# Moving the projection's two-input GpSimd steps to VectorE and giving the low-rank sigmoids their own priority in a hybrid SGU, convolution and RWKV-7 block

## The chip, the cores and the metric

One core of one Trainium2 chip runs the whole kernel. The metric is the device time of one execution in microseconds (us); runs are compared by their medians.

## The reference, cut to what matters

The input `x` has 2048 tokens of 1024 features. All arithmetic is float32.

```python
h = rms_norm(x, pre_norm_g)
z = h @ w_in                                  # 1024 x 3712
out_a = spatial_gating(u_a, v_a, ...) * silu(g_a)
out_b = conv_module(val_b, glu_b, ...) * silu(g_b)      # 31 taps, 256 channels
out_c = rwkv7_mix(z_c, ...) * silu(z_g)                 # a scan over 2048 tokens, 8 heads
x = x + rms_norm(concat(out_a, out_b, out_c) @ w_out, post_norm_g)
x = x + (p @ ple_w) * sigmoid(x @ ple_gate_w + ple_gate_b)
```

Inside `rwkv7_mix` the columns of z are shifted by a token (`z + mu * (prev - z)`), and two of them go through low-rank products:

```python
log_w = -DECAY_SCALE * sigmoid(w0 + tanh(wd) @ w_up)
a     = sigmoid(a0 + ad @ a_up)
kk    = k * k_k;  kk = kk * rsqrt(max(sum(kk * kk), 1e-12))     # per head
k     = k * (1 + (a - 1) * k_a)
```

## The kernel before, in words

The program has three stages: the projection with all that prepares the scan (about 0 to 700 us), the scan over chunks of 64 tokens (to about 1190 us), and the output projection with the gate. The change lies in the first.

The projection works in two halves of 1024 tokens. In each, `s_gemm` computes 29 column tiles of 128 columns in the order of the list `ORDER`; two of them (2 and 3) are computed with tokens on the partitions (`gemm_t`, L312), all others by `gemm` (L300). A matmul takes its operands in the format fp32r; to keep float32 accuracy, h and the weights are split into a high and a low part, and a tile takes 48 matmuls of 128x512 (high by high, high by low and low by high for 8 blocks of k and 2 groups of 512 tokens). The result z of a tile has one of two PSUM buffers, which is free again once ScalarE and VectorE have drained it: `shift` does so by L329, L330 and L336, other tiles by a sigmoid, a product or a silu.

`load_w` brings the weights of a tile in the first half: a DMA of the raw tile (L278), the high part by ScalarE (L282), the low part by GpSimd (L283), and two DMAs that store both parts (L285) for the second half, which loads them ready-made. The pool `w` has six buffers, so two sets of raw, high and low: the parts of a tile are written into buffers that an earlier tile's matmuls have just left.

`build_h` makes h. For the first group of 512 tokens VectorE does all of it (L260, L263). For the other groups the tokens lie already transposed in DRAM, and a two-input product by the row of inverse norms (L268) comes first: by VectorE for even groups, by GpSimd for odd ones. `norm_h` puts that engine into `X[g]`.

Per tile there is further work: the convolution's 31 taps for 1024 tokens and two tiles (`s_conv`, L452 on VectorE), the low-rank products (`s_lora` and `s_prep`: the split L430 on GpSimd, the matmuls L469 and L474, the sigmoids L476 and L478 on ScalarE, then the scan L481 on VectorE and the exponentials L484 and L485), the sums over heads (`parts` L231 and L232, matmuls L240), the root L503 and its reciprocal (`recip`, L245), products with r, k and v (L505 to L546), the transposes L537, and the sums L553. `s_sgu` and `s_pw` do the same for the other branches (L595, L603, L637). `s_const` makes the split of the low-rank weights (L165).

Each of these generators yields times in units of a tile, and `at()` sets the priority of what follows. The framework's scheduler puts all instructions into one list per engine by these priorities and by what it expects of their readiness. On the chip each engine then runs its list strictly in that order.

```python
    at(b0 + TG[24] - 5)
    o = shift(12, half, zz, "mk")
```

The value after `at` is the tile's own place (`TG`) less 5: such a step is put ahead of other work that is ready. Names such as z174 or w171 below are buffers with a running number; z174, z193, z198 and z205 are four consecutive tiles of the first half, w171 is the low part of the weights of z198, w188 that of z205, and mk559 is a low part in the second half's last convolution statistics.

## Time and profile before

| what | us |
|---|---|
| median of 3 runs | 1432.69 |
| the runs | 1432.69, 1432.87, 1430.08 |
| the profiled execution | 1433.92 |
| its span | 1432.2 |
| TensorE busy in the span | 1376.5 |
| VectorE busy | 1009.7 |
| ScalarE busy | 579.2 |
| GpSimd busy | 243.6 |

The profile is of one execution. Its span runs from the first to the last instruction that it shows; the execution's own time is 1.7 us longer. Busy time of an engine is the time in which one of its instructions ran. The idle time before an instruction is put down to the instruction of another engine, or the DMA, that it waited for last. In a timeline equal instructions that follow on one another are merged, with their count behind an x; in a row of waits stand the total, how many there were, and the longest.

### The profile page before, as it was taken

The numbers are of one execution on the slowest core, as the hardware profiler recorded it, in microseconds if no ns is written. First come the engines' busy times: TensorE is split into PE (matmuls) and PEld (weight loads), VectorE is DVE, ScalarE is ACT, GpSimd is POOL, SyncE is SP. The second block draws the span as 40 slices with busy tenths as digits, with TensorE's granted clock in tenths as the row PEclk, the third lists the DMA queues.
The fourth block names the chain that finished last, engine by engine and source line by source line (L and its number), as shares of the span: only waits on it lengthen the run. The fifth ranks groups of instructions, "written<-read, shape, count | busy, mean of one in ns | idle before, by whom it ended". The sixth has DMA issues, their size and how long they took to land.

```text
span 1432.2 us, 24400 instructions
## 1 busy us (share of the span) xinstructions
PE 1376.5 (96%) x9701; PEld 1100.4 (77%) x9701; DVE 1009.7 (71%) x2003; ACT 579.2 (40%) x913; POOL 243.6 (17%) x284
## 2 busy tenths in 40 slices
PE   7998999999999999999899999999998989999998
PEld 6876877787898778778677777777776767888887
DVE  6599994885527999777666597789779544545453
ACT  6334445555332344444333554544553543111121
POOL 5431221221501000000111211211221101111120
PEclk9999999999999999999999899999999999999999
DMA  8432466679534458755822833242331534232331
GB/s 335 147 148 89 144 207 193 189 259 298 207 107 157 173 183 249 221 149 187 251 89 78 318 114 105 86 138 82 124 100 57 167 117 147 100 140 100 121 115 44
DMA packets 158311, 223.29 MB, mean 156 GB/s; under 512 B 58236, under 2 KB 108149, under 8 KB 158198
## 3 DMA queue, kind: packets, MB, share of 16 engines
q1 hardware_dynamic: 158066, 221.68, 47.1%
q8 instruction: 76, 1.25, 0.4%
q14 instruction: 37, 0.30, 0.1%
q10 hardware_dynamic: 132, 0.06, 0.0%
HBM read 132.58 MB, written 89.13 MB: 155 GB/s over the span
## 4 chain that ended last, share of the span: by engine, by line
PE 69%; DVE 24%; ACT 3%; issue 2%; DMA 2%; POOL 0%; ACTq 0%; POOLq 0%; DVEq 0%
PE z L300 32%; PE z L1167 12%; PE z L1054 6%; DVE inv L452 6%; PE c L1144 3%; DVE inv L873 3%; DVE inv L878 3%; PE z L312 2%; PE m L820 2%; PE m L240 1%; DVE mk L245 1%; DVE L L976 1%; DVE inv L861 1%; PE m L1123 1%; PE c L943 1%
## 5 line engine op out<-in xcount | busy, mean ns | idle before, releaser
L300 PE MATMUL z<-h,w 128*128 128x512 f32 x2592 | 631.6, 398 | 1.5 <-ACT zl L336 1.4
L300 PEld LDWEIGHTS z<-h,w 128*128 128x128 f32 x2592 | 485.0, 189 | 119.3 <-issue 6.0
L1054 PE MATMUL z<-h,w 128*128 128x512 f32 x768 | 203.5, 408 | 0.6 <-DVE w L1041 0.6
L452 DVE SCALAR_TENSOR_TENSOR inv<-inv,vc,inv 128x1024 f32<-128x1024 f32 x120 | 171.7, 1449 | 1.4
L1054 PEld LDWEIGHTS z<-h,w 128*128 128x128 f32 x768 | 138.4, 190 | 31.2 <-DVE w L1041 1.0
L283 POOL TENSOR_TENSOR w<-w,w 128x1024 fp32r<-128x1024 f32 x26 | 71.6, 2755 | 238.3 <-PE z L300 172.5
L1167 PE MATMUL z<-L,w 128*128 128x512 f32 (+1 forms) x384 | 96.3, 394 | 0.0
L1151 ACT ACTIVATE inv<-inv 128x512 f32<-128x512 f32 (+1 forms) x33 | 20.5, 620 | 182.1 <-DVE inv L1150 182.1
L1167 PE MATMUL z<-h,w 128*128 128x512 f32 (+1 forms) x384 | 93.1, 390 | 0.8 <-DVE inv L1150 0.8
L873 DVE TENSOR_TENSOR inv<-inv,inv 128x48 f32<-128x48 f32 (+23 forms) x464 | 85.7, 219 | 2.3
L878 DVE TENSOR_TENSOR inv<-inv,inv 128x48 f32<-128x48 f32 (+23 forms) x464 | 84.2, 217 | 1.2
L1167 PEld LDWEIGHTS z<-h,w 128*128 128x128 f32 x384 | 71.3, 188 | 17.4 <-DVE inv L1150 1.2
L1150 DVE TENSOR_TENSOR inv<-z,L 128x512 f32<-128x512 f32 (+1 forms) x32 | 21.8, 683 | 89.1 <-PE z L1167 89.1
L1167 PEld LDWEIGHTS z<-L,w 128*128 128x128 f32 x384 | 70.4, 188 | 15.3
L1111 POOL TENSOR_TENSOR inv<-inv,pg 128x1024 f32<-128x1024 f32 x16 | 38.3, 2397 | 218.0 <-DMA inv<-mx_s 168.1
L245 DVE RECIPROCAL mk<-mk 128x256 f32<-128x256 f32 x40 | 65.8, 1708 | 12.1 <-ACT mk L637 8.0
L825 DVE TENSOR_TENSOR mk<-m,mask 128x512 f32<-128x512 f32 x58 | 37.5, 683 | 35.9 <-PE m L820 31.7
L978 POOL TENSOR_TENSOR ri<-ri,pc 128x256 f32<-128x256 f32 x31 | 19.5, 629 | 236.1 <-DVE L L976 225.9
L312 PE MATMUL z<-w,h 128*128 128x256 f32 x384 | 52.5, 293 | 0.9 <-ACT h L262 0.9
L312 PEld LDWEIGHTS z<-w,h 128*128 128x128 f32 x384 | 50.3, 197 | 3.0 <-ACT h L262 1.6
L829 ACT COPY inv<-mk 32x128 f32<-32x128 f32 x128 | 37.8, 295 | 35.9 <-DVE mk L825 33.1
L282 ACT CAST w<-w 128x1024 fp32r<-128x1024 f32 x26 | 27.3, 1048 | 60.1 <-DMA w<-in_w_in_dram 44.4
(245 smaller groups left out, 1959.0 us busy)
## 6 DMA issues: line engine op xcount, KB each, us to landing
w_s<-w SPq DMA_DIRECT2D x58, 512.0 KB, 3.4
w<-w_s SPq DMA_DIRECT2D x58, 512.0 KB, 5.3
w<-in_w_in_dram SPq DMA_DIRECT2D x26, 512.0 KB, 3.8
L<-in_x_dram SPq DMA_DIRECT2D x16, 512.0 KB, 7.3
ar_s<-L SPq DMA_DIRECT2D x16, 512.0 KB, 4.7
wo_s<-w SPq DMA_DIRECT2D x16, 512.0 KB, 4.5
L<-ar_s SPq DMA_DIRECT2D x32, 256.0 KB, 3.1
L<-bk_s SPq DMA_DIRECT2D x32, 256.0 KB, 3.9
```

Source lines behind the costliest of these rows:

```text
L245: nc.vector.reciprocal(t[:, g * 256:(g + 1) * 256], t[:, g * 256:(g + 1) * 256])
L283: nc.gpsimd.tensor_tensor(out=ws[1], in0=wr, in1=ws[0], op=ALU.subtract)
L300: nc.tensor.matmul(z[:, g * 512:(g + 1) * 512], lhsT=ws[a][:, k * 128:(k + 1) * 128], rhs=h[:, b, k, :], start=(n == 0), stop=(n == 23))
L312: nc.tensor.matmul(z[:, i * 256:(i + 1) * 256], lhsT=h[:, b, k, i * 128:(i + 1) * 128], rhs=ws[k // 4][a][:, (k % 4) * 256:(k % 4 + 1) * 2 ...
L452: nc.vector.scalar_tensor_tensor(out=ac, in0=y[:, i:i + HT], scalar=col(V_CW + 2 * i + ct), in1=ac, op0=ALU.mult, op1=ALU.add)
L829: nc.scalar.copy(g["g"][32 * q:32 * q + 32, 0, 4 * ci:4 * ci + 4, :], mk[32 * q:32 * q + 32, par, :, s0:s0 + 32])
L873: nc.vector.tensor_tensor(out=tmp[:, o:o + n, :m], in0=tl[:, lo:hi, m:m + 1].to_broadcast([128, n, m]), in1=ml[:, m, :m].unsqueeze(1).to_b ...
L878: nc.vector.tensor_tensor(out=tl[:, lo:hi, :m], in0=tl[:, lo:hi, :m], in1=tmp[:, o:o + n, :m], op=ALU.add)
L1054: nc.tensor.matmul(mx[:, nh * 512:(nh + 1) * 512], lhsT=oT[a][:, k, :], rhs=wo[k // 4][:, b, k % 4, nh * 512:(nh + 1) * 512], start=(k == ...
L1111: nc.gpsimd.tensor_tensor(out=x2, in0=x2, in1=pg[0], op=ALU.mult)
L1144: nc.tensor.matmul(pp, lhsT=pT[:, a, k, :], rhs=gw[8 + k][b][:, nh * 512:(nh + 1) * 512], start=(n == 0), stop=(n == 5))
L1167: nc.tensor.matmul(z, lhsT=xT[a][:, k, :], rhs=gw[k][b][:, sl], start=(k == 0 and n == 0), stop=(k == 7 and n == 2))
```

## The change

GpSimd's four kinds of two-input instructions in the projection become VectorE's: the split of the low-rank weights (L165), the product L268 of odd groups, the weight split L283 and the split L430. In `s_prep` the two sigmoids are given the priority of the tile's place less 5, and the priority goes back to its old value behind them.

```diff
--- before.py
+++ after.py
@@ -162,7 +162,7 @@
             hi = slice(64 * j, 64 * j + 64)
             for lo in (0, 64):
                 nc.scalar.copy(wup_h[lo:lo + 64, j], wup_t[hi])
-            nc.gpsimd.tensor_tensor(out=wup_l[hi], in0=wup_t[hi], in1=wup_h[hi, j], op=ALU.subtract)
+            nc.vector.tensor_tensor(out=wup_l[hi], in0=wup_t[hi], in1=wup_h[hi, j], op=ALU.subtract)
         nc.sync.dma_start(out=pw_t, in_=pw_w.rearrange("(k p) n -> p k n", p=128))
         yield 1.5
         cps = mps((128, 2, 128))
@@ -223,7 +223,7 @@
             nc.sync.dma_start(out=xk, in_=x_t[256 * k2:256 * k2 + 256, g * 512:(g + 1) * 512]
                               .rearrange("(k p) t -> p k t", p=128))
             xt += [xk[:, 0], xk[:, 1]]
-        X[g] = (xt, rb[:, 1], nc.vector if g % 2 == 0 else nc.gpsimd)
+        X[g] = (xt, rb[:, 1])
 
     def parts(src, eng):
 
@@ -262,10 +262,10 @@
                     nc.scalar.copy(h[:, 0, k4, sl], xb)
                     nc.vector.tensor_tensor(out=h[:, 1, k4, sl], in0=xb, in1=h[:, 0, k4, sl], op=ALU.subtract)
             return h
-        xt, rb, eng = xr
+        xt, rb = xr
         for k in range(8):
             at(t + 0.05 * k)
-            eng.tensor_tensor(out=xt[k], in0=xt[k], in1=rb, op=ALU.mult)
+            nc.vector.tensor_tensor(out=xt[k], in0=xt[k], in1=rb, op=ALU.mult)
             nc.scalar.activation(h[:, 0, k, :], xt[k], AF.Identity, scale=col(V_PRE + k))
             nc.vector.scalar_tensor_tensor(out=h[:, 1, k, :], in0=xt[k], scalar=col(V_PRE + k),
                                            in1=h[:, 0, k, :], op0=ALU.mult, op1=ALU.subtract)
@@ -280,7 +280,7 @@
         for wr, ct in zip(wrs, cts):
             ws = [new("w", dt=F32R) for _ in range(2)]
             nc.scalar.copy(ws[0], wr)
-            nc.gpsimd.tensor_tensor(out=ws[1], in0=wr, in1=ws[0], op=ALU.subtract)
+            nc.vector.tensor_tensor(out=ws[1], in0=wr, in1=ws[0], op=ALU.subtract)
             for j in range(2):
                 nc.sync.dma_start(out=w_s[ct, :, j], in_=ws[j].bitcast(F32))
             r.append(ws)
@@ -427,7 +427,7 @@
             wa = new(tag, dt=F32R)
             hi, lo = slice(64 * j, 64 * j + 64), slice(64 - 64 * j, 128 - 64 * j)
             nc.scalar.copy(wa[hi], o[hi])
-            nc.gpsimd.tensor_tensor(out=wa[lo], in0=o[hi], in1=wa[hi], op=ALU.subtract)
+            nc.vector.tensor_tensor(out=wa[lo], in0=o[hi], in1=wa[hi], op=ALU.subtract)
             st["wa"].append(wa)
 
     def s_conv(half, ct, st):
@@ -473,9 +473,12 @@
                 hi = slice(64 * j, 64 * j + 64)
                 nc.tensor.matmul(lps[j], lhsT=wup_l[hi, p * 128:(p + 1) * 128], rhs=wa[j][hi, sl],
                                  start=False, stop=True)
+
+            at(b0 + TG[12 + p] - 5)
             nc.scalar.activation(sw[:, 8 * g:8 * g + 8, 1:65], lps[0].rearrange("p (c s) -> p c s", s=64),
                                  AF.Sigmoid, bias=col(V_W0 + p))
             nc.scalar.activation(ic[:, g * 512:(g + 1) * 512], lps[1], AF.Sigmoid, bias=col(V_A0 + p))
+            at(b0 + TG[12 + p] - 0.6)
 
         ep = sw
         nc.vector.tensor_tensor_scan(ep.rearrange("p c s -> p (c s)"), rst.rearrange("p c s -> p (c s)"),
```

Lines up to 475 are the same in both kernels; from there the changed kernel's numbers are larger by 2 or 3 (L501 becomes L504, L503 L506, L537 L540, L546 L549, L553 L556, L595 L598).

The first place is in the first half, behind the end of z174, on VectorE. Before, the list went by L517 and the drain of z167 to the clamp L501 of the head sums and the reciprocals:

```order
L452 SCALAR_TENSOR_TENSOR inv105_894<-inv104_890,vc_116,inv105_894 128x1024
L232 TENSOR_TENSOR mk154_1303<-mk152_1300,mk153_1302 128x1024
L452 SCALAR_TENSOR_TENSOR inv105_894<-inv104_890,vc_116,inv105_894 128x1024
L517 TENSOR_TENSOR L172_1433<-L139_1155,L128_1070 128x8x64
L330 SCALAR_TENSOR_TENSOR L168_1419<-z167_1369,vc_116,L168_1419 128x1023
L452 SCALAR_TENSOR_TENSOR inv105_894<-inv104_890,vc_116,inv105_894 128x1024 x2
L501 TENSOR_SCALAR mk152_1300<-m155_1306 128x512
L501 TENSOR_SCALAR mk152_1300<-m156_1310 128x512
L452 SCALAR_TENSOR_TENSOR inv105_894<-inv104_890,vc_116,inv105_894 128x1024
L245 RECIPROCAL mk152_1300<-mk152_1300 128x256 x4
L452 SCALAR_TENSOR_TENSOR inv105_894<-inv104_890,vc_116,inv105_894 128x1024
L232 TENSOR_TENSOR mk164_1353<-L117_979,mk163_1352 128x1024
```

Now:

```order
L232 TENSOR_TENSOR mk154_1303<-mk152_1300,mk153_1302 128x1024
L529 TENSOR_TENSOR L112_916<-L122_1044,L112_916 128x1024
L549 SCALAR_TENSOR_TENSOR L117_979<-L117_979,vc_116,L122_1044 128x1024
L452 SCALAR_TENSOR_TENSOR inv105_894<-inv104_890,vc_116,inv105_894 128x1024 x2
L283 TENSOR_TENSOR w171_1428<-w169_1425,w170_1427 128x1024
L504 TENSOR_SCALAR mk152_1300<-m155_1306 128x512
L504 TENSOR_SCALAR mk152_1300<-m156_1310 128x512
L452 SCALAR_TENSOR_TENSOR inv105_894<-inv104_890,vc_116,inv105_894 128x1024 x2
L245 RECIPROCAL mk152_1300<-mk152_1300 128x256 x4
L452 SCALAR_TENSOR_TENSOR inv105_894<-inv104_890,vc_116,inv105_894 128x1024
L232 TENSOR_TENSOR mk164_1353<-L117_979,mk163_1352 128x1024
L283 TENSOR_TENSOR w188_1547<-w186_1544,w187_1546 128x1024
```

The split of w171 stands ahead of the clamp, and that of w188 behind the reciprocals. On ScalarE the root L503 (now L506), which these reciprocals need, stood ahead of the cast of w187:

```order
L336 COPY zl_126<-z167_1369 128x1
L503 ACTIVATE mk152_1300<-mk152_1300 128x1024
L539 COPY mk157_1328<-m158_1329 128x512
L231 CAST mk163_1352<-L117_979 128x1024
L539 COPY mk157_1328<-m159_1335 128x512
L282 CAST w187_1546<-w186_1544 128x1024
```

Now:

```order
L336 COPY zl_126<-z167_1369 128x1
L282 CAST w187_1546<-w186_1544 128x1024
L506 ACTIVATE mk152_1300<-mk152_1300 128x1024
L542 COPY mk157_1328<-m158_1329 128x512
L231 CAST mk163_1352<-L117_979 128x1024
L542 COPY mk157_1328<-m159_1335 128x512
```

The cast has moved ahead of the root, the two copies L539 and the high part L231.

The second place is where VectorE's list comes to the drain of z193. Before:

```order
L525 TENSOR_TENSOR mk152_1300<-mk152_1300,L134_1090 128x1024
L523 TENSOR_TENSOR L151_1296<-L151_1296,mk129_1071 128x1024
L481 SCALAR_TENSOR_TENSOR L179_1520<-inv1_98,L179_1520 128x1040
L452 SCALAR_TENSOR_TENSOR inv105_894<-inv104_890,vc_116,inv105_894 128x1024
L526 TENSOR_TENSOR L134_1090<-L151_1296,L134_1090 128x1024
L546 SCALAR_TENSOR_TENSOR L139_1155<-L139_1155,vc_116,L151_1296 128x1024
L330 SCALAR_TENSOR_TENSOR L194_1619<-z193_1569,vc_116,L194_1619 128x1023
L232 TENSOR_TENSOR mk190_1554<-L139_1155,mk189_1553 128x1024
```

Now, with the third split and the gate product of z198 ahead of that drain:

```order
L528 TENSOR_TENSOR mk152_1300<-mk152_1300,L134_1090 128x1024
L526 TENSOR_TENSOR L151_1296<-L151_1296,mk129_1071 128x1024
L484 SCALAR_TENSOR_TENSOR L179_1520<-inv1_98,L179_1520 128x1040
L452 SCALAR_TENSOR_TENSOR inv105_894<-inv104_890,vc_116,inv105_894 128x1024
L529 TENSOR_TENSOR L134_1090<-L151_1296,L134_1090 128x1024
L549 SCALAR_TENSOR_TENSOR L139_1155<-L139_1155,vc_116,L151_1296 128x1024
L283 TENSOR_TENSOR w197_1627<-w195_1624,w196_1626 128x1024
L598 TENSOR_TENSOR mk175_1495<-z198_1636,mk175_1495 128x1024
L452 SCALAR_TENSOR_TENSOR inv105_894<-inv104_890,vc_116,inv105_894 128x1024
L330 SCALAR_TENSOR_TENSOR L194_1619<-z193_1569,vc_116,L194_1619 128x1023
L232 TENSOR_TENSOR mk190_1554<-L139_1155,mk189_1553 128x1024
```

So w197's split, L598 (before L595) and a tap come between L549 and L330, and L595 stood behind L232 before.

The third place is the end of the second half on TensorE, where the last sums of the convolution statistics (mk559, L240) stand. Before, with matmuls of the tile z588 behind them:

```order
L300 MATMUL z588_4922<-h346_2839,w545_4650 128x512
L300 MATMUL z588_4922<-h346_2839,w544_4649 128x512 x2
L240 MATMUL m561_4741<-mk559_4737,onesm_84 128x512
L240 MATMUL m562_4747<-mk559_4737,onesm_84 128x512
L300 MATMUL z588_4922<-h346_2839,w545_4650 128x512
L300 MATMUL z588_4922<-h346_2839,w544_4649 128x512 x2
L300 MATMUL z588_4922<-h346_2839,w545_4650 128x512
L300 MATMUL z588_4922<-h346_2839,w544_4649 128x512 x2
L300 MATMUL z588_4922<-h346_2839,w545_4650 128x512
L300 MATMUL z588_4922<-h346_2839,w544_4649 128x512 x2
L300 MATMUL z588_4922<-h346_2839,w545_4650 128x512
L300 MATMUL z588_4922<-h346_2839,w544_4649 128x512
L537 MATMUL m569_4833<-ident_78,L553_4724 128x128 x4
```

Now, with all of these ahead of them:

```order
L300 MATMUL z588_4922<-h346_2839,w545_4650 128x512
L300 MATMUL z588_4922<-h346_2839,w544_4649 128x512 x2
L300 MATMUL z588_4922<-h346_2839,w545_4650 128x512
L300 MATMUL z588_4922<-h346_2839,w544_4649 128x512
L240 MATMUL m561_4741<-mk559_4737,onesm_84 128x512
L240 MATMUL m562_4747<-mk559_4737,onesm_84 128x512
L540 MATMUL m569_4833<-ident_78,L553_4724 128x128 x4
L540 MATMUL m570_4839<-ident_78,L553_4724 128x128 x4
L240 MATMUL m573_4852<-mk571_4848,ones64_83 128x512
```

What follows both is the transposes L537 (L540) and the last sums over heads.

## Rows read from the trace of the kernel before

**Rows 1.** The page's busy line: busy us of each engine, share of the span, instructions.
```profile
PE 1376.5 (96%) x9701; PEld 1100.4 (77%) x9701; DVE 1009.7 (71%) x2003; ACT 579.2 (40%) x913; POOL 243.6 (17%) x284
```

**Rows 2.** TensorE's waits, 36 to 250 us: what it waited for, us in total, times, longest.
```profile
PE m L240 <- ACT mk L231: 3.6, 2, 2.7
PE m L240 <- DVE mk L232: 1.7, 1, 1.7
PE z L300 <- ACT zl L336: 1.4, 1, 1.4
PE c L469 <- ACT L L476: 0.3, 1, 0.3
```

**Rows 3.** Two windows at half clock: start:end, length, busy us (instructions) by engine, clock, DMA.
```profile
143.50:146.90 3.40, 3.40 (x9) 2.75 (x9) 3.40 (x3) 1.07 (x2) 0.77 (x1) 0.50 0.00 0
...
696.50:703.30 6.80, 4.73 (x42) 4.40 (x44) 4.33 (x7) 3.48 (x3) 0.00 (x0) 0.50 0.95 265
```

**Rows 4.** GpSimd's groups by form: count, busy us, mean ns, idle before, releasers.
```profile
L283 POOL TENSOR_TENSOR w<-w,w 128x1024 fp32r<-128x1024 f32 x26 | 71.6, 2755 | 238.3 <-PE z L300 172.5 <-ACT w L282 55.2 <-DMA bk_s<-mk 7.0
L268 POOL TENSOR_TENSOR L<-L,mk 128x512 f32<-128x512 f32 x16 | 26.0, 1658 | 13.5 <-DMA w_s<-w 13.5
...
L430 POOL TENSOR_TENSOR pg<-mk,pg 64x1024 fp32r<-64x1024 f32 x2 | 6.5, 3273 | 0.1
...
L165 POOL TENSOR_TENSOR yc<-mk,ri 64x512 fp32r<-64x512 f32 x2 | 2.9, 1442 | 0.2
```

**Rows 5.** VectorE's groups by form, same columns.
```profile
L452 DVE SCALAR_TENSOR_TENSOR inv<-inv,vc,inv 128x1024 f32<-128x1024 f32 x120 | 171.7, 1449 | 1.4
...
L232 DVE TENSOR_TENSOR mk<-mk,mk 128x1024 fp32r<-128x1024 f32 x12 | 14.6, 1220 | 8.5 <-ACT mk L231 8.0 <-PE m L240 0.4
...
L553 DVE TENSOR_TENSOR L<-m,L 128x512 f32<-128x512 f32 x16 | 10.3, 683 | 8.7 <-PE m L240 8.7
```

**Rows 6.** VectorE's timeline around 182 us: start, length, instruction.
```profile
181.02 3.42 DVE L546 SCALAR_TENSOR_TENSOR L<-L,vc,L 128x1024 f32<-128x1024 f32 x1
```

**Rows 7.** GpSimd's timeline, 160 to 226 us: start, length, instruction, idle before and releaser.
```profile
180.07 3.28 POOL L283 TENSOR_TENSOR w<-w,w 128x1024 fp32r<-128x1024 f32 x1 [7.05 <-DMA bk_s<-mk]
195.30 2.40 POOL L283 TENSOR_TENSOR w<-w,w 128x1024 fp32r<-128x1024 f32 x1 [11.95 <-PE z L300]
```

**Rows 8.** Windows of the first 700 us, columns as in Rows 3.
```profile
184.00:226.00 42.00, 39.05 (x168) 29.43 (x168) 39.21 (x35) 23.66 (x28) 7.25 (x4) 1.00 0.71 205
...
250.00:430.00 180.00, 180.00 (x885) 146.44 (x884) 109.30 (x109) 82.79 (x103) 42.37 (x20) 1.00 0.63 212
430.00:680.00 250.00, 250.00 (x1094) 197.59 (x1093) 209.69 (x204) 101.97 (x106) 9.06 (x10) 1.00 0.61 188
```

**Rows 9.** VectorE's timeline in the head, 0 to 40 us.
```profile
10.05 3.23 DVE L263 TENSOR_TENSOR h<-L,h 128x512 fp32r<-128x512 f32 x2
```

**Rows 10.** ScalarE's timeline, 186 to 215 us.
```profile
199.36 1.05 ACT L282 CAST w<-w 128x1024 fp32r<-128x1024 f32 x1 [2.83 <-DMA w<-in_w_in_dram]
```

**Rows 11.** VectorE's timeline, 188 to 222 us.
```profile
194.66 6.59 DVE L245 RECIPROCAL mk<-mk 128x256 f32<-128x256 f32 x4
...
215.56 2.31 DVE L481 TENSOR_TENSOR_SCAN L<-inv,L 128x1040 f32<-128x1040 f32 x1
...
221.30 1.27 DVE L330 SCALAR_TENSOR_TENSOR L<-z,vc,L 128x1023 f32<-128x1023 f32 x1
```

**Rows 12.** TensorE's timeline, 200 to 228 us.
```profile
225.92 2.25 PE L300 MATMUL z<-h,w 128*128 128x512 f32 x9
```

**Rows 13.** TensorE's timeline, 680 to 700 us.
```profile
687.29 2.73 PE L300 MATMUL z<-h,w 128*128 128x512 f32 x11
```

**Rows 14.** TensorE's waits, 640 to 710 us, columns as in Rows 2.
```profile
PE m L240 <- DVE mk L232: 2.6, 1, 2.6
PE m L603 <- DVE L L553: 2.1, 1, 2.1
PE m L240 <- ACT mk L231: 1.2, 1, 1.2
```

## The prediction, made before the changed kernel ran

> **What bounds the kernel now.** The page's busy line comes first: TensorE works 96% of the span, VectorE 71%, GpSimd 17% [rows 1]. The change touches the projection stage (0 to about 700 us) alone, so only what TensorE misses there can be won: its waits and its time at a lower clock. The waits of TensorE from 36 to 250 us sum to 3.6 + 1.7 + 1.4 + 0.3 = 7.0 us, and each ends on VectorE or on ScalarE work that stood behind VectorE [rows 2]. After the longest wait the granted clock is 0.50 for 3.4 us, the 1.2 GHz level instead of 2.4, with TensorE busy throughout, which loses half of it, 1.7 us [rows 3]. So 8.7 us are to be had in the first half. From 250 to 680 us TensorE is busy without a gap while VectorE has 71 and 40 us free [rows 8]: there an instruction more on VectorE costs nothing. At the end of the second half there are 2.6 + 2.1 + 1.2 = 5.9 us of waits [rows 14] and 6.8 us at 0.50 [rows 3].
>
> Why VectorE is late in the first half is read from two timelines side by side. L546 starts at 181.02 and takes 3.42 us; the weight split L283 on GpSimd runs from 180.07 to 183.35 [rows 6, 7]. For the same amount of data VectorE takes 1.2 to 1.3 us elsewhere (L232 1.22, L330 1.27) [rows 5, 11]. The same shows in the means: the 120 convolution taps L452 average 1.449 us, 0.18 above 1.27, hence 120 x 0.18 = 21 us lost by them alone [rows 5].
>
> **The change part by part.** Removed from GpSimd are 29 splits L283 (26 of 2.755 us, three more of the head), 16 steps L268 of 1.658, four L430 and two L165 [rows 4]. VectorE gets them at its own prices, 1.22 us for 128x1024 (L232) and 0.68 for 128x512 (L553) [rows 5]: 29 x 1.22 + 16 x 0.68 + 4 x 1.22 + 2 x 0.68 = 52.5 us. It gets back at least the 21 us of the taps; at most it gets back the moved instructions' whole GpSimd time, 71.6 + 26.0 + 2 x 6.5 + 2.9 and some 7 for the head's three splits = about 120 us, if VectorE had stood still through all of it. The busy sum thus does not decide. The Trainium skill (Perfetto Trace Analysis, Optimizing Scalar/DVE Operations) says that moving work between GpSimd and VectorE might not help, as they share a read port; by that alone the change would be worth about nothing, and rows 6 and 7 agree that they block one another. What decides is where the added instructions stand in VectorE's queue.
>
> *Up to the end of tile z174 (about 195 us).* I laid VectorE's new order end to end with the durations above, letting each L283 wait for the end of the gemm whose buffer it reuses, as GpSimd's did (172.5 us in all [rows 4]). The drains L330 of z116, z121 and z138 then come 6 us or more before TensorE needs their buffers, and so do the sums of L240. All waits before this point go: 1.41 and 2.67, the 1.70 behind L232 [rows 2], and the 1.7 us of clock [rows 3]: -7.5 us.
>
> *From the end of z174 to the start of z205.* Here a wait comes instead. On GpSimd the split of w171 waited 11.95 us for the end of z174 and ended nobody's work [rows 7]. Now it stands on VectorE ahead of L501 (first fence of the change); what is queued behind it are L501, the taps, the reciprocals L245, and 20 more instructions until L330 of z193 frees the buffer that z205 needs (second fence). With tau = 0 at z174's end (195.30 [rows 7]), 1.2 us for each full step and 0.6 for a half one: split, two L501, two taps, 4.8. L245 needs ScalarE's L503, which now stands behind the cast of w187, whose data came at 199.36, tau 4.1 [rows 10]; 4.1 + 1.05 + 1.06 = 6.2. L245 6.6 [rows 11], 12.8. Then tap, L232, split, L505, tap: 18.8. Three halves, tap, L521, two halves: 24.3. Tap, L525, L523: 27.9; the scan 2.3 [rows 11]: 30.2; tap, L526, L546, the third split, L595, tap: 37.4; L330: 38.6. Starts overlap a little, so I take 38 us. Before, L330 of z193 started at tau 26.0 [rows 11] and z205 at 30.6 [rows 12], of which 0.29 + 0.96 = 1.25 were waits [rows 2]; z205 could start at 29.35 were VectorE in time. The new wait is 38 - 29.35 = 8.7 us, less those 1.25: **+7.4 us**. It lies open, because the c and m matmuls ahead of z205 wait on ScalarE behind the same scan. The bounds: 6 us (all starts overlapping, L503 in time) and 10.
>
> *The clock in that wait.* No row shows what an 8.7 us wait does to it; 2.7 us was followed by 3.4 us at 0.50, the 5.9 us by 6.8 us [rows 3]. Half of these is 1.7 and 3.4; I take **+2.5**, keeping 0 to 3.4.
>
> *Head.* Three splits now stand between the steps that make h: 3 x 1.22 = 3.7 us more. Without GpSimd beside them two L263 that took 3.23 us [rows 9] take 1.3, and one L202 wins about as much: 3.8 us less. I take **0**, -1.5 to +1.5.
>
> *End of the second half.* The pair L240 of mk559 stood ahead of 11 matmuls L300 that took 2.73 us [rows 13]; now it stands behind them (third fence). From this pair hang L637, L245, L232 and L603, which are waited for in the open [rows 14], and the 11 matmuls no longer fill any of it: 11 x 0.23 = **+2.5 us**, 0 to +4.
>
> *The rest.* L268 of the second half and L430 of the second half lie in 250 to 680 us, covered by VectorE's free 71 and 40 us [rows 8]; they would cost at most 8 x 0.68 + 2 x 1.22 = 7.9 us if that cover were gone. L165 has VectorE idle around it. The stores of the low parts (L285) follow the splits on SP's queue, later by at most the new wait; they are read again in the second half, hundreds of us later. GpSimd's queue keeps only memsets. The sigmoids L476/L478 move by one or two places on ScalarE, behind the same matmuls: 0, with -1 to +1.
>
> Sum: -7.5 + 7.4 + 2.5 + 0 + 2.5 = **+4.9 us**. The profiled execution took 1433.92 us (span 1432.2, so 1.7 around it); with the change 1438.8. That execution is 1.2 above the median of 1432.69, so I forecast 1437.6. With the bounds, 1433.5 to 1442.
>
> **The rivals.**
> (1) *VectorE set free.* The Trainium skill (SBUF — State Buffer, SBUF: two separate sides) has it that a VectorE instruction with two SBUF operands and a GpSimd one that reads SBUF exclude each other for a whole instruction. Rows 6 and 7 agree. As a mechanism of this kernel: if blocked time is most of what VectorE was late by, the tau chain ends before tau 30, all 8.7 us go, and with the +2.5 at the end the time is 1432.69 - 6.2 = 1426.5. For it: VectorE was 93% busy from 184 to 226 us (39.21 of 42) [rows 8]. Against it: the chain above already uses unblocked durations. 0.23.
> (2) *Every split a wait.* Each L283 of the first half holds VectorE's queue until a gemm ends; if a gemm's worth of VectorE work exceeds the 11 us between two ends not once but at two or three tiles, the wait of z205 comes again. One more is +8.7 and clock: 1447. It decides from the point where VectorE is still behind when z205 ends; after it VectorE had much idle time, so 0.12.
> (3) *The two cancel.* The chain ends at tau 33 to 35, by a start earlier than I see: then -7.5 + 3 + 2.5 + a little clock = about -1, 1431.7. This is also the case that the change does little because TensorE's matmuls moved to later places. 0.15.
>
> **How the numbers follow.** The forecast has 0.5. A measurement of this kernel can tell about 0.2%, 2.9 us, from no change. Faster: rival 1 and a little of 3, 0.25. Same: most of 3 and the lower end of the forecast, 0.21. Slower: the rest of the forecast and rival 2, 0.54. The range from 1426 to 1443 takes in rivals 1 and 3 and leaves out rival 2 and the tails.
>
> **What would show it.** Right: in the trace of the changed kernel no tap L452 above 1.4 us; no TensorE wait from 100 to 185 us and no 0.50 there; VectorE waiting for TensorE ahead of L283; an idle stretch of TensorE of 7 to 10 us ahead of z205, ended by L330, L231 or the sigmoid of c184, near 220 us; the waits at 690 us at about 8.5. Wrong: z205 starting by 219 us with no such gap (rival 1); a second such gap after 240 us (rival 2).

## The result, and the profile after

The changed kernel takes 1440.35 us (median of 4 runs, 1439.07 to 1441.86); the kernel before, run again beside it, 1432.78 us. The ratio is 1.0061 [1.0046, 1.0076], so it is slower by 0.6%. The forecast of 1437.6 us had the direction, and its range holds the time. The profiled execution took 1439.07 us with a span of 1437.4, 5.2 us more than the span before. The busy line of the page, as in [rows 1]:

```profile
PE 1376.4 (96%) x9701; PEld 1100.4 (77%) x9701; DVE 1005.8 (70%) x2054; ACT 582.6 (41%) x915; POOL 123.9 (9%) x233
```

GpSimd's busy time falls from 243.6 to 123.9 us, while VectorE, with 51 instructions more, is busy for 3.9 us less. Two groups of VectorE's lines by form show the larger part of why (count, busy us, mean ns, idle time ahead and what ended it):

```profile
L452 DVE SCALAR_TENSOR_TENSOR inv<-inv,vc,inv 128x1024 f32<-128x1024 f32 x120 | 151.0, 1277 | 1.2
...
L283 DVE TENSOR_TENSOR w<-w,w 128x1024 fp32r<-128x1024 f32 x26 | 31.8, 1222 | 30.8 <-PE z L300 9.4 <-PE z L312 9.4 <-issue 6.6
```

The 120 taps fall from 1449 to 1277 ns [rows 5], 120 x 0.172 = 20.7 us given back; 26 splits come in at 1.22 us, 31.8 us. What outweighs the rest is spread over other steps that GpSimd no longer holds up: the eight L549, for one, take 10.2 us in all where they took 14.5 as L546. The second row holds the price that the busy time hides: VectorE stands idle for 30.8 us ahead of splits, 18.8 of them for the gemm whose weight buffer they reuse.

TensorE's waits from 36 to 250 us (what it waited for, us in total, times, longest), as in [rows 2]:

```profile
PE c L469 <- ACT mk L480: 4.7, 1, 4.7
PE z L300 <- ACT mk L595: 3.5, 1, 3.5
PE m L240 <- ACT mk L231: 1.8, 1, 1.8
PE z L312 <- ACT mk L438: 1.1, 1, 1.1
```

They sum to 11.1 us against 7.0. The 2.7, 1.7 and 1.4 of before are gone; the 0.3 + 1.0 ahead of z205 have become 4.7 + 1.8, and the 3.5 ahead of z198 is new. These three lie on TensorE's way from z174 to z205. Its timeline there (start, length, instructions, idle time ahead and what ended it):

```profile
195.82 1.03 PE L540 MATMUL m<-ident,L 128*128 128x128 f32 x8
...
204.79 6.23 PE L300 MATMUL z<-h,w 128*128 128x512 f32 x19 [3.52 <-ACT mk L595]
...
226.18 0.80 PE L469 MATMUL c<-mk,ri 128*128 128x512 f32 x1 [4.68 <-ACT mk L480]
...
229.49 1.22 PE L240 MATMUL m<-mk,ones 128*128 128x512 f32 x2 [1.80 <-ACT mk L231]
230.51 3.68 PE L300 MATMUL z<-h,w 128*128 128x512 f32 x11
```

z174 ended at 188.32 (195.40 before), so the forecast's tau is the time less 188.2, the start of the split behind it. From there VectorE's timeline, same columns:

```profile
188.19 1.23 DVE L283 TENSOR_TENSOR w<-w,w 128x1024 fp32r<-128x1024 f32 x1 [1.49 <-PE z L300]
...
194.35 6.59 DVE L245 RECIPROCAL mk<-mk 128x256 f32<-128x256 f32 x4 [1.22 <-ACT mk L506]
...
215.97 2.32 DVE L484 TENSOR_TENSOR_SCAN L<-inv,L 128x1040 f32<-128x1040 f32 x1
...
225.18 1.27 DVE L330 SCALAR_TENSOR_TENSOR L<-z,vc,L 128x1023 f32<-128x1023 f32 x1
```

The split waits 1.49 us for z174, as forecast; the reciprocals start at tau 6.2 (forecast 6.2), the scan at 27.8 (27.9), L330 of z193 at 37.0 (37.4). But L330, which ended at 226.45, is not what ended the waits. ScalarE's timeline shows what did:

```profile
196.46 0.59 ACT L542 COPY mk<-m 128x512 f32<-128x512 f32 x1 [2.15 <-PE m L540]
...
202.42 1.28 ACT L595 ACT_TABLE_LOAD   x1 [3.95 <-DMA v_s<-mk]
...
219.10 0.59 ACT L542 COPY mk<-m 128x512 f32<-128x512 f32 x1 [4.03 <-PE m L540]
...
222.06 1.06 ACT L487 ACTIVATE L<-L 128x1024 f32<-128x1024 f32 x1
...
225.44 0.69 ACT L480 ACTIVATE mk<-c,vc 128x512 f32<-128x512 f32 x1
...
228.41 1.03 ACT L231 CAST mk<-L 128x1024 fp32r<-128x1024 f32 x1
```

The silu L595 that drains the z buffer for z198 waits 3.95 us for the store v_s to free an mk buffer. That store reads the copies L542, and those wait for the transposes L540, which TensorE now reaches later in its list. So z198 starts 3.52 us late. Further on the copy L542 waits 4.03 us for the next transposes, and L487 (which needs the scan), L480 and L231 follow it in ScalarE's queue: they end TensorE's 4.68 and 1.80. z205 starts at 230.51, tau 42.3; before it was 225.92 [rows 12].

Windows of the four stretches up to 715 us in which the granted clock was 0.50, the 1.2 GHz level (start:end, length, busy us and instructions by engine, clock, DMA share, GB/s), as in [rows 3]:

```profile
41.50:44.90 3.40, 3.29 (x8) 1.99 (x7) 3.30 (x8) 0.99 (x2) 0.00 (x0) 0.50 0.00 0
205.30:208.70 3.40, 3.40 (x9) 2.69 (x9) 3.40 (x6) 2.69 (x3) 0.00 (x0) 0.50 0.86 324
225.80:232.60 6.80, 4.62 (x9) 3.05 (x10) 3.74 (x4) 4.73 (x7) 0.00 (x0) 0.50 0.75 231
700.30:713.90 13.60, 7.74 (x52) 5.96 (x53) 11.13 (x12) 4.58 (x4) 0.00 (x0) 0.50 0.66 189
```

One stretch follows each wait or group of waits; the first (41.50) stands in the head. At the end of the second half TensorE's waits, as in [rows 14]:

```profile
PE m L240 <- DVE mk L232: 4.2, 1, 4.2
PE m L606 <- DVE L L556: 1.6, 1, 1.6
PE m L240 <- ACT mk L231: 1.0, 1, 1.0
PE m L540 <- ACT mk L640: 0.6, 1, 0.6
```

That is 7.4 us where 5.9 stood, and 13.6 us at half clock where 6.8 stood.

The account of the two profiled executions, by the start of the same work (us, before and after):

| work on TensorE | before | after | change so far |
|---|---|---|---|
| z85 | 55.62 | 57.40 | +1.8 |
| z138 | 128.14 | 128.11 | 0.0 |
| end of z174 | 195.40 | 188.32 | -7.1 |
| z205 | 225.92 | 230.51 | +4.6 |
| the gemm at the end of the first half | 360.82 | 367.48 | +6.7 |
| the last gemm ahead of the waits at 690 us | 677.33 | 684.13 | +6.8 |
| the next gemm behind them | 708.85 | 718.61 | +9.8 |
| end of the span | 1432.18 | 1437.35 | +5.2 |

The 4.6 us that come back after 709 us lie in code that the change doesn't touch. From that next gemm to the end it took 723.3 us before, 718.7 after, and 720.3 to 723.9 in the profiles of the experiments below, so it varies between executions. Its last 2 us left out, it held 17.1 us at 0.50 before and 10.2 after, which with TensorE busy is up to 3.4 of the 4.6 us; the rest lies in its short waits and isn't traced further. So the profiles differ by 5.2 us where the medians differ by 7.6: the profiled execution of the kernel before lay 1.1 us above its median, that of the changed kernel 1.3 below.

### The profile page after: what moved, and what is told of

Same layout as the page of the kernel before. It is cut to its first block, busy times and chain, and to the rows that moved or that the text cites. A ratio compares the mean times of both kernels' runs of the same rounds, so it can differ in the third digit from the quotient of the medians.

```text
span 1437.4 us, 24384 instructions
## 1 busy us (share of the span) xinstructions
PE 1376.4 (96%) x9701; PEld 1100.4 (77%) x9701; DVE 1005.8 (70%) x2054; ACT 582.6 (41%) x915; POOL 123.9 (9%) x233
## 3 DMA queue, kind: packets, MB, share of 16 engines
q8 instruction: 76, 1.25, 0.4%
## 4 chain that ended last, share of the span: by engine, by line
PE 79%; DVE 14%; ACT 4%; DMA 2%; issue 1%; SPq 0%; ACTq 0%; DVEq 0%
PE z L300 41%; PE z L1170 12%; PE z L1057 6%; DVE inv L876 3%; PE z L312 3%; PE c L1147 3%; DVE inv L881 3%; PE m L823 2%; PE m L240 1%; DVE L L979 1%; DVE inv L864 1%; PE m L1126 1%; PE c L946 1%; DMA w<-in_gate_w_dram 1%; PE c L474 1%
## 5 line engine op out<-in xcount | busy, mean ns | idle before, releaser
L452 DVE SCALAR_TENSOR_TENSOR inv<-inv,vc,inv 128x1024 f32<-128x1024 f32 x120 | 151.0, 1277 | 1.2
L245 DVE RECIPROCAL mk<-mk 128x256 f32<-128x256 f32 x40 | 65.9, 1709 | 20.2 <-ACT mk L506 11.1
L329 ACT ACTIVATE L<-z,om 128x1024 f32<-128x1024 f32 x24 | 26.8, 1115 | 85.8 <-PE z L300 85.8
L282 ACT CAST w<-w 128x1024 fp32r<-128x1024 f32 x26 | 27.3, 1050 | 77.9 <-DMA w<-in_w_in_dram 58.4
L283 DVE TENSOR_TENSOR w<-w,w 128x1024 fp32r<-128x1024 f32 x26 | 31.8, 1222 | 30.8 <-PE z L300 9.4
```

Source lines behind the costliest of these rows:

```text
L245: nc.vector.reciprocal(t[:, g * 256:(g + 1) * 256], t[:, g * 256:(g + 1) * 256])
L452: nc.vector.scalar_tensor_tensor(out=ac, in0=y[:, i:i + HT], scalar=col(V_CW + 2 * i + ct), in1=ac, op0=ALU.mult, op1=ALU.add)
```

## The experiments

The theory, called queue theory in the expectations: list order decides. A two-input step on VectorE takes less than half the time (a split 1.22 us instead of 2.76), but takes its wait for a gemm along into VectorE's queue, and the order around it changes on all engines. Rivals: VectorE has too much to do in that stretch (capacity), or the sigmoids' new place costs. Ratios are to the kernel before in the same series.

**1. The moves without the sigmoids.**

```diff
-            at(b0 + TG[12 + p] - 5)
             nc.scalar.activation(sw[...], ..., AF.Sigmoid, ...)
             nc.scalar.activation(ic[...], ..., AF.Sigmoid, ...)
-            at(b0 + TG[12 + p] - 0.6)
```

> The changed kernel without the sigmoids' priority; all four kinds of instruction stay on VectorE. Queue theory (the loss comes from where the weight splits stand in VectorE's queue): the lists around z174 to z205 are those of the changed kernel, so 1440 us within 2 us, a gap of about 10 us ahead of z205 in all (3.5, 4.7 and 1.8 in the trace of the change). Sigmoid theory (the earlier sigmoids hold up ScalarE's casts and roots there): 1433 us or less, with the 4.7 us wait behind the second sigmoid gone.

Measured: 1439.04 us, 1.0041 [1.0025, 1.0056]. TensorE's waits from 36 to 250 us are the changed kernel's to a tenth of a us: 4.7, 3.5, 1.8 and 1.1.

z205 starts at 228.53; the 3.4 us at half clock at 41.5 us are missing here, and z85 starts at 55.44, so the head itself costs nothing. The sigmoids' priority doesn't bring these waits; it moves nothing at all. In the two traces TensorE, VectorE, ScalarE and GpSimd run the same operations on the same tiles (by their names without the numbers) in the same order from the first to the last.

**2. The sigmoids alone** (the kernel before with their priority).

```diff
+            at(b0 + TG[12 + p] - 5)
             nc.scalar.activation(sw[...], ..., AF.Sigmoid, ...)
             nc.scalar.activation(ic[...], ..., AF.Sigmoid, ...)
+            at(b0 + TG[12 + p] - 0.6)
```

> The kernel before with the sigmoids' priority alone. Queue theory: as before, 1433 us within 2 us, with the waits of 1.4, 2.7 and 1.7 us in the first half still there. Sigmoid theory: slower by 3 us or more, with a wait behind L480 ahead of z205.

Measured: 1432.88 us, 0.9998 [0.9987, 1.0008]. The order on all four engines is that of the kernel before. So that part of the change does nothing, and the whole loss is the moves'. The waits that were expected again are there only in part: the 1.4 us for L336 are missing and the longest for L231 is 3.4 us, not 2.7, so some of a profile's waits differ between executions of the same lists.

**3. The changed kernel with the splits L283 on GpSimd.**

```diff
-            nc.vector.tensor_tensor(out=ws[1], in0=wr, in1=ws[0], op=ALU.subtract)
+            nc.gpsimd.tensor_tensor(out=ws[1], in0=wr, in1=ws[0], op=ALU.subtract)
```

> The changed kernel with the weight splits L283 back on GpSimd; the 16 products, the splits of the low-rank product and of its weights stay on VectorE. Queue theory: the gap ahead of z205 goes (waits there of 1 to 2 us as before), the waits of the kernel before at 126 to 185 us come back in part because GpSimd blocks VectorE again, and the end of the second half keeps its later pair L240 (+3 us): 1433 to 1437 us. Capacity theory (VectorE simply has too much work): between the two as well, about 1435, but with the gap ahead of z205 only shortened. Where the end of the second half has waits of about 6 us as before, its 3 us came from the splits.

Measured: 1437.29 us, 1.0034 [1.0022, 1.0047], at the upper end of what the queue theory gave. The waits behind L480 and L595 are gone, but waits of 4.0 (1.7 of them right ahead of z205), 1.1, 1.1 and 1.1 us stand at other places, the taps are back at 1423 ns, and the end of the second half has 7.6 us of waits, so its loss doesn't come from the splits. They are not the whole loss: L268, L430 and the rest, moved without them, cost 0.34% (4.9 us). In this profile 2.1 us of that arise at the end of the second half and about as much in the first 70 us, where 3.4 us stand at half clock.

**5. The splits alone on VectorE** (the kernel before, one line).

```diff
-            nc.gpsimd.tensor_tensor(out=ws[1], in0=wr, in1=ws[0], op=ALU.subtract)
+            nc.vector.tensor_tensor(out=ws[1], in0=wr, in1=ws[0], op=ALU.subtract)
```

> The kernel before with all 29 weight splits on VectorE and nothing else moved. The split of w171 now stands behind L501, the cast of w187 behind the root, and L330 of z193 comes some 6 us sooner after the end of z174 than in the changed kernel; the last pair L240 of the second half keeps its 11 matmuls behind it. Queue theory: the 7 us won before z174's end stay, 3 us of waits remain ahead of z205, nothing is lost at the end of the second half: 1428 to 1432 us. Capacity theory (35 us more work on VectorE, wherever it stands): 1437 to 1440 us.

Measured: 1440.09 us, 1.0041 [1.0024, 1.0057]; the gain that I expected was missed. z205 starts at 220.62 as it should. The loss stands 160 us later. TensorE's timeline there, then VectorE's:

```profile
383.11 11.10 PE L300 MATMUL z<-h,w 128*128 128x512 f32 x36 [5.87 <-DVE w L283]
```
```profile
368.32 12.53 DVE L268 TENSOR_TENSOR L<-L,mk 128x512 f32<-128x512 f32 x8 [8.08 <-ACT mk L219]
380.77 2.28 DVE L283 TENSOR_TENSOR w<-w,w 128x1024 fp32r<-128x1024 f32 x1
```

and GpSimd's beside it:

```profile
368.86 13.11 POOL L268 TENSOR_TENSOR L<-L,mk 128x512 f32<-128x512 f32 x8 [32.13 <-ACT mk L219]
```

A split stands behind eight L268 that run beside GpSimd's eight (12.53 us for eight; in the changed kernel one L268 takes 0.69 us), itself takes 2.28 us beside GpSimd, and a gemm waits 5.87 us for it; 6.8 us at half clock go with it. The forecast looked at no such place. It is not the second rival's mechanism either: this split does not hold VectorE's queue for a gemm, it is late because of what stands ahead of it. With experiment 3 the two parts make 0.34% + 0.41%, and both together 0.61%; the intervals are too wide to tell whether they add, but the stalls of the parts stand for the most part at other places than those of the whole.

The start of z205 shows something more: here the splits of w171, w188 and w197 are VectorE's too, and it comes at 220.62. They delay z205 in the order that they have with the other moves, not by being on VectorE.

**4 and 8. Which splits.** The changed kernel with the splits of the first half from step 15 on back on GpSimd (4), and with those of steps 15 to 17 alone back (8):

```diff
-            nc.vector.tensor_tensor(out=ws[1], in0=wr, in1=ws[0], op=ALU.subtract)
+            (eng or nc.vector).tensor_tensor(out=ws[1], in0=wr, in1=ws[0], op=ALU.subtract)
...
-                    W[0, ct] = load_w(ct, tag="inv" if n == 2 else "w")
+                    W[0, ct] = load_w(ct, tag="inv" if n == 2 else "w",
+                                      eng=nc.gpsimd if n >= 15 else None)
```

(in 8: `nc.gpsimd if 15 <= n <= 17 else None`)

> The changed kernel, but the weight splits from the tile z198 on (14 of 29) are GpSimd's, the first 15 VectorE's. Queue theory: the waits from 100 to 185 us stay away and the 10 us of waits ahead of z205 fall to 0 to 2 us with their 5 us at half clock: 1440 - 10 - 2.5 = 1427 to 1430 us. Capacity theory: VectorE gives up only 3.5 us of work before z205, so the gap falls by about 3.5 us: 1436 us.

> The changed kernel with only three of its 29 splits back on GpSimd, those of w171, w188 and w197, which stand between the ends of z174 and z198. Queue theory: those three make the gap, so this equals the run with 14 late splits on GpSimd (1432 us) within 1.5 us. Capacity theory: 3 x 1.2 us of VectorE's time come back, at most 4 us: 1436 us.

Measured: 1432.29 us, 0.9996 [0.9985, 1.0007], and 1438.77 us, 1.0032 [1.002, 1.0044]. z205 starts at 219.50 and 219.63, some 9 us earlier than in experiment 1, whose head has no half clock either: sending three splits back takes the delay of z205 away. But both still have 5.7 us of waits before 250 us and the loss at 690 us. So 4 misses the 1427 to 1430 us: 6.4 us ahead of the kernel before at z205, it is 3.3 us ahead at 674 us, and the end of the second half takes 2.6 of these. And 8, which I expected within 1.5 us of 4, loses some 5.6 us at the end of the first half: the gemm there starts 3.9 us later than in 4, and 3.4 us at half clock stand behind it. TensorE's timeline of 8 there, then ScalarE's:

```profile
354.43 1.98 PE L665 MATMUL c<-inv,jk 128*128 128x512 f32 x4
360.38 6.45 PE L300 MATMUL z<-h,w 128*128 128x512 f32 x20 [3.97 <-ACT pg L657]
```
```profile
354.20 1.04 ACT L282 CAST w<-w 128x1024 fp32r<-128x1024 f32 x1 [6.51 <-DMA w<-in_w_in_dram]
358.01 1.28 ACT L657 ACT_TABLE_LOAD   x1 [2.76 <-DMA ab_s<-pg]
359.31 1.02 ACT L657 ACTIVATE pg<-z 128x1024 f32<-128x1024 f32 x1
```

L657 drains the buffer that the gemm at 360.38 needs, and stands behind a cast whose weights came late and a store that frees pg. In the changed kernel the same wait is 1.4 us, in 4 it is 0.2. Moving three splits changed the order 140 us later.

**11. Capacity or order.** The changed kernel with the splits of steps 15 to 17 made twice. The second writes the same values.

```diff
-            nc.vector.tensor_tensor(out=ws[1], in0=wr, in1=ws[0], op=ALU.subtract)
+            for _ in range(times):
+                nc.vector.tensor_tensor(out=ws[1], in0=wr, in1=ws[0], op=ALU.subtract)
...
-                    W[0, ct] = load_w(ct, tag="inv" if n == 2 else "w")
+                    W[0, ct] = load_w(ct, tag="inv" if n == 2 else "w", times=2 if 15 <= n <= 17 else 1)
```

> The changed kernel with the splits of w171, w188 and w197 made twice, which changes no value: 3.5 us more work on VectorE between z174's end and z205. Capacity theory: the drain of z193 ends 3.5 us later, at 230 us, and the run takes 1443 to 1445 us. Queue theory: the time follows what the lists put ahead of z205; here the scheduler leaves the root ahead of the cast of w187 again and puts the pair L240 of z205's head sums behind 31 matmuls of z205, so z205 starts right behind the drain, at 227 to 230 us and not later than in the changed kernel: 1437 to 1441 us.

Measured: 1439.3 us, 1.0052 [1.004, 1.0064]. With more work on VectorE L330 of z193 starts at 220.51 and z205 at 226.03, about 1 us earlier than expected. In experiment 1, which like this run has no half clock at 41.5 us, they start at 223.20 and 228.53. TensorE's waits, line numbers one higher:

```profile
PE c L470 <- ACT mk L481: 5.0, 2, 3.7
PE z L301 <- ACT mk L596: 3.5, 1, 3.5
```

Capacity falls: it asked for a z205 that is 3.5 us later, and more work there gave an earlier one, partly because the pair L240 of z205's head sums now stands behind its first matmuls. The added instructions led to another order on the engines, and that order decided; the 3.5 us of z198 stay. The time itself can't be told from the changed kernel's (0.52% against 0.61%).

**6 and 7. A part of the moves.** The kernel before with the splits of steps 4 to 14 and L430 of the first half on VectorE (6); the same with L430 of the second half too (7: `nc.vector` for both halves):

```diff
-            nc.gpsimd.tensor_tensor(out=ws[1], in0=wr, in1=ws[0], op=ALU.subtract)
+            (eng or nc.gpsimd).tensor_tensor(out=ws[1], in0=wr, in1=ws[0], op=ALU.subtract)
...
-                    W[0, ct] = load_w(ct, tag="inv" if n == 2 else "w")
+                    W[0, ct] = load_w(ct, tag="inv" if n == 2 else "w",
+                                      eng=nc.vector if 4 <= n < 15 else nc.gpsimd)
...
-            nc.gpsimd.tensor_tensor(out=wa[lo], in0=o[hi], in1=wa[hi], op=ALU.subtract)
+            (nc.vector if half == 0 else nc.gpsimd).tensor_tensor(out=wa[lo], in0=o[hi], in1=wa[hi], op=ALU.subtract)
```

> The kernel before with the splits of the 11 tiles from n = 4 to 14 of the list and the first half's split L430 on VectorE; all else stays on GpSimd, the later splits too. Both losses that the queue theory names are left out: no split stands in VectorE's queue after z174, and the last pair L240 keeps its place. Queue theory: 1424 to 1428 us, the fastest of all. If a loss of another kind goes with the moves (the head, VectorE's load), 1431 or more.

> As the run before it, with the second half's L430 on VectorE too, two instructions more. They are covered by VectorE's free time; but the scheduler then puts the last pair L240 behind all 11 matmuls of its tile. If the place of that pair costs the 3 us at the end of the second half, this run is 2.5 to 3.5 us above the run before it, with the TensorE waits near 690 us at 7.5 instead of 6 us; if not, the two are equal.

Measured: 1432.64 us, 0.9994 [0.9984, 1.0003], and 1434.74 us, 1.0009 [1.0, 1.0018]. 6 misses its gain: waits of 1.8, 1.6 and 1.2 us stand before 250 us and one of 1.5, for a split on GpSimd, later. Its lead over the kernel before is 4.0 us at z205, 2.1 at the end of the first half and nothing at 677 us. 7 is a clean test of the forecast's last term, since it differs from 6 by two instructions. TensorE's timeline at the end of the second half, of 6 and then of 7:

```profile
686.82 0.61 PE L240 MATMUL m<-mk,onesm 128*128 128x512 f32 x2
687.28 2.73 PE L300 MATMUL z<-h,w 128*128 128x512 f32 x11
...
695.69 0.74 PE L240 MATMUL m<-mk,ones 128*128 128x512 f32 x2 [2.65 <-DVE mk L232]
```
```profile
686.07 2.25 PE L300 MATMUL z<-h,w 128*128 128x512 f32 x9
688.16 0.62 PE L240 MATMUL m<-mk,onesm 128*128 128x512 f32 x2
...
697.03 1.22 PE L240 MATMUL m<-mk,ones 128*128 128x512 f32 x2 [4.44 <-DVE mk L232]
```

In 6 the last pair L240 stands ahead of 11 matmuls, in 7 behind them; the wait for L232 grows from 2.65 to 4.44 us. From the last gemm ahead of these waits to the next one behind them it takes 31.5 and 34.0 us, so +2.5, and the medians differ by 2.1, a little less than the 2.5 to 3.5 expected. All other profiles agree: the same stretch takes 33.6 to 34.5 us in the seven with the second half's L430 on VectorE (the changed kernel, 1, 3, 4, 7, 8, 11) and 30.5 to 31.7 in the six that keep it on GpSimd (the kernel before, 2, 5, 6, 9, 10; 12, which moves the pair itself, is apart).

**9 and 10. Raw weights in another pool.** The splits wait because raw weights and their parts share the pool w. Here the raw weights come from pool L, in 9 for steps up to 14 (splits of steps 4 to 14 on VectorE, all else as before), in 10 for the whole first half with every split on VectorE (`"inv" if n == 2 else "L"`). The edit of 9, whose `eng` does the split as in 6:

```diff
-                    W[0, ct] = load_w(ct, tag="inv" if n == 2 else "w")
+                    W[0, ct] = load_w(ct, tag="inv" if n == 2 else "L" if n < 15 else "w",
+                                      eng=nc.vector if 4 <= n < 15 else nc.gpsimd)
```

> The kernel before with the splits of tiles n = 4 to 14 on VectorE, and the raw weights of tiles up to n = 14 in the pool L instead of w, so that the six buffers of w hold three sets of high and low parts there and a split need not wait for the gemm two tiles back. If the idle time of VectorE ahead of its splits (4.5 of the 9 us in the changed kernel between z85's end and the drain of z193) is what keeps the gain from arriving, that idle time falls below 1.5 us, z205 starts at 216 to 219 us and the run takes 1427 to 1430 us. If VectorE's work in that stretch sets the end whatever the waits, z205 starts at 220 to 222 as in the runs with early splits only, and the run takes 1431 to 1433 us.

> The kernel before with all 29 splits on VectorE and the raw weights in L throughout. In the run with all splits on VectorE and raw weights in w, TensorE waited 5.9 us for a split that stood behind eight products L268 at 381 us. Queue theory: that split can now stand ahead of them, and z205 starts at 217 to 220 us: 1428 to 1432 us instead of 1440. If loads into L come late because the buffers of L are held by the scan's operands, TensorE waits for weights instead, and the run takes 1436 us or more.

Measured: 1430.66 us, 0.9986 [0.9978, 0.9995], and 1437.47 us, 1.0035 [1.0023, 1.0047]. In 9 VectorE's idle time ahead of its splits, from 64 us to the drain of z193, falls to 1.0 us from 9.0 in the changed kernel, and still z205 starts at 220.13, where the other theory wanted it; the time lies between the two ranges. But VectorE doesn't set that start either. L330 of z193 starts at 213.78 and takes 1.28 us, 5 us ahead of z205. The waits that are left before 250 us are for ScalarE:

```profile
PE m L240 <- ACT mk L231: 2.4, 1, 2.4
PE c L470 <- ACT mk L479: 1.4, 1, 1.4
```

From 250 to 640 us there is none. In 10 the wait of experiment 5 at 383 us is gone, as expected, but z205 starts at 222.52, and the time is in the range of the second theory for another reason: the cast L282 at the end of the first half waits 10.0 us for a gemm (not for late weights), a drain stands behind it, and TensorE waits 3.4 us for that.

**12. The end of the second half, earlier.** 9, and the statistics of the second half's last tiles get earlier due times:

```diff
-        yield b0 + NG - 8.5
+        yield b0 + NG - (8.5 if half == 0 else 9.3)
...
-        yield b0 + NG - 7.6
+        yield b0 + NG - (7.6 if half == 0 else 8.6)
...
-        yield b0 + NG - 7.0
+        yield b0 + NG - (7.0 if half == 0 else 8.0)
```

> The run with raw weights in L and early splits on VectorE, with the second half's convolution statistics given priorities 0.8 to 1 tile earlier. The last pair L240 of these statistics now has 22 matmuls L300, eight transposes and 12 more L300 behind it before TensorE needs what hangs from it, 34 x 0.23 = 7.8 us of work instead of 2.5. If the 5.5 to 6 us of TensorE waits at the end of the second half (and 3.4 of the 6.8 us at half clock behind them) hang from the place of this pair alone, they fall to 1 to 2 us and the run takes 1424 to 1427 us. If another chain (the head sums L232 and L553) ends there as late, 1428 to 1431 us.

Measured: 1421.43 us (1418.95 to 1423.71), 0.9914 [0.9895, 0.9933]: faster than both kernels, and better than expected. TensorE's timeline at the end of the second half:

```profile
678.87 0.63 PE L240 MATMUL m<-mk,onesm 128*128 128x512 f32 x2
...
684.44 1.03 PE L538 MATMUL m<-ident,L 128*128 128x128 f32 x8
685.23 3.03 PE L300 MATMUL z<-h,w 128*128 128x512 f32 x12
688.10 1.09 PE L240 MATMUL m<-mk,ones 128*128 128x512 f32 x4
690.80 1.97 PE L604 MATMUL m<-yc,mk 128*64 128x128 f32 x32 [1.60 <-DVE L L554]
```

The pair L240 and the transposes now stand ahead of 22 and 12 matmuls that fill their waits; of 5.5 us in 9 one wait of 1.60 is left, and the 6.8 us at half clock at 690 us are gone. Up to 615 us this profiled execution of 12 is 2.0 us behind that of 9, by 3.4 us more at half clock at 54 us and 3.4 more at 218 us in the same order; from there to the next gemm behind these waits it gains 6.5 us. The last stage gives 1.9 more, so that the two spans differ by 6.4 us. The medians differ by 9.2, since the profiled execution of 9 lay 1.5 us below its median and that of 12 1.0 above. The due times alone, on the kernel before, were not tried, so what the new pool of 9 adds to the 0.86% isn't known.

## Why the prediction was right

The direction was right, and so was the kind of mechanism: what is won ahead of z174's end is lost again ahead of z205 and at the end of the second half. The size owes something to luck. At 709 us the profile had lost 9.8 us where the sum had 4.9, and 4.6 came back by the variation of an unchanged stage; the medians differ by 7.6. And the range, 17 us wide, would have held two of the rivals as well.

- **Contention** [rows 5, 6]: forecast 21 us back on the taps, measured 20.7, and it did not decide, as the forecast said. The rule of the Trainium skill (Perfetto Trace Analysis, Optimizing Scalar/DVE Operations), that such a move might not help, fits the result, but not for want of a freer VectorE: the order took more than the port gave.
- **Up to the end of z174, -7.5 us:** measured -7.1. The waits of [rows 2] are gone, and none stands from 100 to 185 us. The -7.1 holds 1.8 us that z85 began late, for the stretch at 41.5 us; experiment 1, with the same lists and without that stretch, has -9.0. A little of it is order: the pair L240 and eight transposes, about 1.25 us of TensorE's time, now come behind z174, and four matmuls of the low-rank products, about 0.8 us, ahead of its end.
- **The new wait, +7.4, and its clock, +2.5, so +9.9:** measured 4.6 + 7.1 = 11.7 us to the start of z205. The windows from z174's end to there, before and after, as in [rows 3]:

```profile
195.40:225.92 30.52, 29.27 (x122) 21.66 (x122) 27.77 (x24) 20.71 (x24) 7.15 (x4) 1.00 0.75 220
188.32:230.51 42.19, 32.19 (x129) 24.03 (x128) 37.46 (x33) 23.65 (x27) 0.13 (x1) 0.90 0.63 187
```

  TensorE's idle time in them grows from 1.25 to 10.0 us, so +8.75. Its busy time grows by 2.9: about 0.4 for the matmuls that changed places, which leaves about 2.5 for the half clock, as forecast. VectorE's chain was right to half a us at every point. What failed is the step "z205 could start at 29.35 were VectorE in time": it let z205 start as L330 ends and took TensorE's way there to be free otherwise. L330 ended at 226.45, and z205 started 4.1 us later. The rows of before show this already: L330 ended at 222.57 [rows 11] and z205 started at 225.92 [rows 12], 3.3 us later. ScalarE's chain (L542 behind the later transposes, then L487, L480, L231) ended later than L330, and the silu wait of z198 was not seen at all. L231 and the sigmoid were named as ends of the wait, and they were; but the one stretch near 220 us is three waits between 201 and 230 us.
- **The head, 0:** 0 in experiment 1. The 1.8 us in the changed kernel's profile come from 3.4 us at half clock which the same order in experiment 1 doesn't have.
- **The sigmoids, 0:** right, though the forecast had them move by a place or two; they don't move (1, 2).
- **The end of the first half** was put at nothing; it cost 1.4 us in a wait for L656. Experiments 8 and 10 show waits of 4.0 and 3.4 us at the same place. The 71 free us of VectorE [rows 8] are no cover there, since the wait comes through ScalarE's order. Nor do they always cover an instruction on VectorE, as experiment 5 shows at 383 us.
- **The end of the second half, +2.5:** +3.0, and +2.5 by experiment 7. Its waits came to 7.4 us where about 8.5 were named, but 6.8 us more at half clock were not in the sum.
- **What lies behind, 0:** -4.6 in the profile, by variation between executions. At the next gemm behind the waits at 690 us the change had cost 9.8.
- **The rivals.** VectorE set free: not so, z205 starts at 230.5 where that rival wanted it by 219 us. Every split a wait: no second gap stands behind 240 us in this kernel. The two cancel: experiments 4 and 6 land there, with fewer steps moved.

Shown: the sigmoid part is without effect (1, 2); the splits of steps 15 to 17 delay z205 in the order that they have with the other moves (4, 8), and not in that of experiment 5; VectorE's capacity doesn't (11); the end of the second half is the order of one pair (7, 12). Less than shown: why z198's silu is late. It follows the transposes, through the copies and the v_s store, by 7.8 to 7.9 us in nine other profiles too (1, 4, 6 to 12), with the transposes starting 1.4 to 7.7 us behind the start of z193; in 5 it is 9.7. But no run moved the transposes alone.

## What to carry to other kernels

Before moving work to a faster engine, look for what that work waits for: the wait goes along, and all that is queued behind it on the new engine waits too. Lay the new order of every engine that hands something on end to end from the first wait, not only of the engine that gets the work. Where a scheduler sets the order, a small move changes it far away, so test the parts by themselves: here 11 splits moved, with raw weights in another pool and three due times changed, gave 0.9%.

## What was not expected of the hardware

Stretches at half clock come in one execution and not in another of the same order: 3.4 us at 41.5 us in the changed kernel, none there in experiment 1, whose lists are the same on all four engines; a wait of 1.4 us in the kernel before is missing in experiment 2 in the same way; and an unchanged stage of some 720 us took 718.7 to 723.9 us. A difference of 5 us between two profiles of this kernel thus needs a stage table before it is put down to a cause. And a taken-away neighbour helps the one that stays as well: with GpSimd's two-input work gone from the projection the taps ran at 1277 ns, the length of an L330 without contention [rows 11].
